# Moving one tile's attention under a different gather, and one tile's weighted sums onto one engine

## Chip, cores, metric

The kernel runs on one core of one Trainium2 chip. The metric is device time in microseconds (us) of one execution, the median over several runs. A core has five engines, each with a queue that it works through in order: TensorE (PE: matmuls; PEld is its weight loads), VectorE (DVE), ScalarE (ACT), GpSimd (POOL, which here only issues the gathers) and SyncE (SP, which issues all other transfers). Sixteen DMA engines move the data.

## The reference, cut to what matters

512 tokens of width 1024 go through two layers. The work is cut into four tiles of 128 tokens.

1. First layer, attention ("mix"): neighbourhood attention and grouped-query attention over all 512 tokens, two sigmoid gates (`ga`, `gb`), two projections, an output projection, added to the tokens.
2. First layer, PEER: each token picks 8 heads x 16 = 128 of 16,384 experts by two rounds of top-16, and adds the gated sum over them:

```python
uc = u[ic]                                            # 128 rows of 1024 for each token
act = einsum("cd,ced->ce", xc, uc)
hid = gelu(act) * gc
out = einsum("ce,ced->cd", hid, v[ic])                # 128 more rows of 1024
```

3. Second layer: a gated state-space block with short convolutions and dense projections (below: "block C"), over the tiles in order.

All inputs are fp32. The rows of `u` and `v` lie side by side, so one gather fetches, for each of 128 tokens, one row of 2048 floats: 128 x 8 KB = 1.049 MB. There are 4 x 128 = 512 such gathers, 537 MB in all.

## The kernel before, in words

**Stages.** `mix_first` does keys and values of all tokens and attention of tile 0. Then `queries` ranks tile 0's experts. `mix_rest([1, 2, 3])` does attention of the other three tiles together: each weight block is loaded once and multiplied with 384 columns (q, `ga`, `gb` and `pj` blocks), then `merge` projects. Then `queries` of tile 1, `queries` of tiles 2 and 3 together (256 columns), the ranking of tiles 2 and 3, and block C for tiles 0 and 1 (`block_c([0, 1])`). When that is through, `T.drain()` does what gathers are left, and `block_c([2, 3])` runs alone.

**The gathers** run beside all this. `peers` is a generator: one step issues two gathers (L269) and all that hangs on them. For each gather: VectorE multiplies the `u` half with the token and sums it up (L271), ScalarE takes Gelu (L276), VectorE makes a diagonal matrix `dg` of the weight (L280), and TensorE multiplies it with the `v` half into two banks of PSUM (L285). `acc` stands for these sums. Four matmuls of 64 x 64 by 512 columns stand for one gather of tiles 1 to 3; each fp32 matmul is two records in the trace, so a gather is eight records.

**Tile 0 is done another way.** A pair of gathers shares four matmuls, which take only the first 512 columns of both `v` rows. The other 512 columns are summed on VectorE into `own` (L295), with weights `hid` (L289):

```python
V.scalar_tensor_tensor(own, g[:, 1, HALVES[1]], hid[:, j:j + 1], own, op0=OP.mult, op1=OP.add)
```

**Pace.** `Paced` counts the columns that TensorE is given (four for one in fp32) and takes a step of `peers` each time `every` columns are full: `PACE_B` during `mix_rest` and tile 1's `queries`, `PACE_Q` during the queries of tiles 2 and 3, `PACE_C` in block C. In the ranking of tiles 2 and 3, `T.steps_now(3)` takes three steps after each head. Then `while 1 not in pre: T.steps_now(1)` takes steps until tile 1's sums have been added to the tokens (`folded`), which the first matmul of block C (`xbc`) needs. A gather needs a free buffer of six (`g`), and buffers come free when the last reader is through.

**Order.** The Tile scheduler reorders what is near; the order on each engine is then fixed. Constants of block C (`cw`, `cb`, `ssn` and others) are loaded when the ranking's memory comes free.

## Time and profile before

| | us |
|---|---|
| median of 3 runs | 2217.51 |
| lowest, highest | 2215.78, 2218.11 |
| the profiled execution, its own time | 2217.67 |
| its span in the trace | 2215.8 |

The page of the profile gives, over the span: PE busy 1851.5 us (84%), DVE 1628.1 (73%), ACT 735.1 (33%), POOL 598.8 (27%); 711.71 MB moved. A busy share is an average over stages with different limits, so the trace is best read in stretches cut where the kernel's stages change. In such a row, the POOL count after 204 us is the number of gathers issued there, since POOL issues nothing else.

### The profile page before, as it was taken

The numbers are of one execution on the slowest core, as the hardware profiler recorded it, in microseconds if no ns is written. First come the engines' busy times: TensorE is split into PE (matmuls) and PEld (weight loads), VectorE is DVE, ScalarE is ACT, GpSimd is POOL, SyncE is SP. The second block draws the span as 40 slices with busy tenths as digits, with TensorE's granted clock in tenths as the row PEclk, the third lists the DMA queues.
The fourth block names the chain that finished last, engine by engine and source line by source line (L and its number), as shares of the span: only waits on it lengthen the run. The fifth ranks groups of instructions, "written<-read, shape, count | busy, mean of one in ns | idle before, by whom it ended". The sixth has DMA issues, their size and how long they took to land.

```text
span 2215.8 us, 29509 instructions
## 1 busy us (share of the span) xinstructions
PE 1851.5 (84%) x10292; PEld 1032.5 (47%) x10292; DVE 1628.1 (73%) x4007; ACT 735.1 (33%) x1471; POOL 598.8 (27%) x520
## 2 busy tenths in 40 slices
PE   7998699899999898656648886896899866799998
PEld 5767445444444654001104552462453421298896
DVE  5376986788885966888868887886775766687865
ACT  4374265566501421111123342321220310154443
POOL 0000223333331233444433334433423333200000
PEclk9999789999999998656758997998999976699999
DMA  5366979889997899999989989899999999653363
GB/s 211 127 228 216 363 288 344 335 325 350 346 381 273 316 378 394 380 380 397 362 306 346 418 365 396 335 418 420 406 415 416 402 416 421 276 170 97 119 189 121
DMA packets 127316, 711.71 MB, mean 321 GB/s; under 512 B 15168, under 2 KB 18752, under 8 KB 61248
## 3 DMA queue, kind: packets, MB, share of 16 engines
q0 software_dynamic: 73728, 536.90, 60.6%
q1 hardware_dynamic: 53440, 172.92, 22.1%
q8 instruction: 83, 1.36, 0.2%
q14 instruction: 65, 0.53, 0.1%
HBM read 707.67 MB, written 2.10 MB: 320 GB/s over the span
## 4 chain that ended last, share of the span: by engine, by line
PE 36%; DMA 25%; DVE 24%; issue 7%; ACT 6%; POOL 1%; another core or an unknown queue 0%; DVEq 0%; POOLq 0%; ACTq 0%; SPq 0%
DMA g<-in_uv,idx 23%; DVE g L271 9%; PE sc L168 5%; PE acc L285 4%; PE mix L168 3%; PE pq L168 2%; PE ga L168 2%; PE z L168 2%; DVE dg L280 2%; PE pg L168 2%; PE ys L168 2%; DVE ww L354 2%; POOL g L269 1%; DVE own L295 1%; PE xbc L168 1%
## 5 line engine op out<-in xcount | busy, mean ns | idle before, releaser
L269 POOL DMA_INDIRECT g<-in_uv,idx x512 | 595.0, 1162 | 1297.7 <-PE acc L285 610.2
L285 PE MATMUL acc<-g,dg 64*64 64x512 f32 x3584 | 626.5, 755 | 249.9 <-DVE dg L280 229.8
L271 DVE SCALAR_TENSOR_TENSOR g<-g,xnp 128x1024 f32<-128x1024 f32 x512 | 624.7, 1221 | 188.2 <-DMA g<-in_uv,idx 181.9
L285 PEld LDWEIGHTS acc<-g,dg 64*64 64x64 f32 x3584 | 122.9, 154 | 621.0 <-DVE dg L280 492.8
L276 ACT ACTIVATE act<-act 128x1 f32<-128x1 f32 (+1 forms) x448 | 90.8, 203 | 945.7 <-DVE g L271 912.2
L354 DVE TENSOR_TENSOR ww<-w,ww 128x1024 fp32r<-128x1024 f32 x175 | 213.4, 1222 | 76.4 <-ACT ww L353 74.5
L280 DVE TENSOR_SCALAR dg<-two,act,gate 128x64 f32<-128x64 f32 x512 | 172.1, 351 | 132.6 <-ACT act L276 129.9
L353 ACT CAST ww<-w 128x1024 fp32r<-128x1024 f32 x175 | 182.2, 1044 | 172.8 <-PE sc L168 63.6
L168 PEld LDWEIGHTS sc<-hT,ww 128*128 128x128 f32 x1536 | 190.0, 193 | 54.0 <-issue 44.5
L168 PE MATMUL sc<-hT,ww 128*128 128x256 f32 x1536 | 206.1, 289 | 6.0 <-ACT fold L333 3.2
L168 PE MATMUL pq<-xT,w 128*128 128x128 f32 (+1 forms) x768 | 127.8, 323 | 0.6 <-DMA w<-in_wq 0.6
L168 PEld LDWEIGHTS pq<-xT,w 128*128 128x128 f32 x768 | 112.0, 200 | 19.8 <-issue 12.2
L295 DVE SCALAR_TENSOR_TENSOR own<-g,hid,own 128x512 f32<-128x512 f32 x127 | 95.1, 749 | 2.3
L168 PE MATMUL ga<-h,w 128*128 128x384 f32 x256 | 93.1, 513 | 2.8 <-DVE rot L411 2.8
L276 ACT ACT_TABLE_LOAD x61 | 78.3, 1283 | 18.1 <-DVE g L271 16.3
L168 PE MATMUL xbc<-hT,ww 128*128 128x256 f32 x480 | 64.2, 290 | 6.2 <-DVE ww L354 3.3
L168 PEld LDWEIGHTS xbc<-hT,ww 128*128 128x128 f32 x480 | 59.3, 192 | 20.4 <-issue 9.5
L168 PEld LDWEIGHTS ga<-h,w 128*128 128x128 f32 x256 | 48.7, 198 | 37.6 <-issue 8.3
L168 PE MATMUL q<-h,w 128*128 128x128 f32 (+1 forms) x256 | 61.1, 394 | 3.4 <-ACT rsq L407 3.4
L168 PE MATMUL mix<-w,ycat 128*128 128x512 f32 x128 | 61.5, 612 | 0.0
L168 PEld LDWEIGHTS z<-hT,ww 128*128 128x128 f32 x384 | 46.9, 190 | 12.3 <-issue 10.5
L168 PE MATMUL z<-hT,ww 128*128 128x256 f32 x384 | 50.5, 287 | 1.5 <-ACT raw L928 1.3
(338 smaller groups left out, 2269.8 us busy)
## 6 DMA issues: line engine op xcount, KB each, us to landing
w<-in_w SPq DMA_DIRECT2D x100, 512.0 KB
w<-in_wq SPq DMA_DIRECT2D x48, 512.0 KB
w<-in_wo SPq DMA_DIRECT2D x32, 512.0 KB
w<-in_wgm SPq DMA_DIRECT2D x16, 512.0 KB
w<-in_wout SPq DMA_DIRECT2D x16, 512.0 KB
g<-in_uv,idx POOLq DMA_INDIRECT x512
w<-in_wpg SPq DMA_DIRECT2D x16, 512.0 KB
w<-in_wqa SPq DMA_DIRECT2D x8, 512.0 KB
```

The source lines that it names most:

```text
L168: return self.count(max(n, 128) * (4 if rhs.dtype == F32 else 1), self.tensor.matmul(out, lhsT, rhs, **kw))
L269: G.indirect_dma_start(out=g.rearrange("p a d -> p (a d)"), out_offset=None, in_=a["uv"], in_offset=bass.IndirectOffsetOnAxis(ap=hk_idx[t] ...
L271: V.scalar_tensor_tensor(g[:, 0, :], g[:, 0, :], 1.0, xnp, op0=OP.mult, op1=OP.mult, accum_out=act[:, j % grp:j % grp + 1])
L276: A.activation(act[:, :grp], act[:, :grp], AF.Gelu)
L280: V.tensor_scalar(dg[:, m, :], two[:, 1, :], act[:, m:m + 1], gate[:, m:m + 1], op0=OP.mult, op1=OP.mult)
L285: T.tensor.matmul(acc[i][o, :], w, v, start=(e0 + j + 1 == grp), stop=(e0 + j + grp >= P), tile_position=(64 * i, 64 * m), skip_group_chec ...
L295: V.scalar_tensor_tensor(own, g[:, 1, HALVES[1]], hid[:, j:j + 1], own, op0=OP.mult, op1=OP.add)
L353: A.copy(ww[:, 0], w)
L354: V.tensor_tensor(ww[:, 1], w, ww[:, 0], op=OP.subtract)
```

## The change

- `mix_rest([1, 2])` (256 columns) stands where `mix_rest([1, 2, 3])` stood; `queries` of tile 1 follows at the same pace `PACE_B`; then `mix_rest([3])` (128 columns) at pace `PACE_Q`. Weights of the mix (`wqa`, `wqb`, `wga`, `wgb`, `wproj`, `wout`) are loaded a second time for tile 3.
- The paces are 10700, 8270 and 4950 instead of 13600, 10500 and 4600.
- Tile 0's sums are done as those of the others: four matmuls for each gather; `own` and `hid` are gone, and so is the form of `folded` for them.
- The ranking of tiles 2 and 3 takes 28 steps instead of 48, and its first two calls of `best` take two heads each.

```diff
-    first, rest = [0], [1, 2, 3]
+    first, late = [0], [2, 3]
-    PACE_B, PACE_Q, PACE_C = 13600, 10500, 4600
+    PACE_B, PACE_Q, PACE_C = 10700, 8270, 4950
...
-                        for m in range(grp):
-                            V.tensor_scalar(dg[:, m, :], two[:, 1, :], act[:, m:m + 1], gate[:, m:m + 1], op0=OP.mult, op1=OP.mult)
-                        for m in range(2):
-                            for i in range(2):
-                                r, o = slice(64 * i, 64 * i + 64), slice(64 * m, 64 * m + 64)
-                                w, v = (dg[r, m, :], gs[m][r, 1, HALVES[0]]) if grp == 2 else (dg[r, 0, :], g[r, 1, HALVES[m]])
...
-                    if t == 0:
-                        hid = sm.tile([P, 2], F32, tag="hid", name="hid", bufs=4)
-                        V.tensor_tensor(hid, act, gate, op=OP.mult)
-                        for j, g in enumerate(gs):
...
-                                V.scalar_tensor_tensor(own, g[:, 1, HALVES[1]], hid[:, j:j + 1], own, op0=OP.mult, op1=OP.add)
...
+                    V.scalar_tensor_tensor(g[:, 0, :], g[:, 0, :], 1.0, xnp, op0=OP.mult, op1=OP.mult, accum_out=act)
+                    A.activation(act, act, AF.Gelu)
+                    dg = dgs()
+                    V.tensor_scalar(dg[:, 0, :], two[:, 1, :], act, hk_gate[t][:, e:e + 1], op0=OP.mult, op1=OP.mult)
+                    for k in range(2):
+                        for i in range(2):
+                            r, o = slice(64 * i, 64 * i + 64), slice(64 * k, 64 * k + 64)
+                            T.tensor.matmul(acc[i][o, :], dg[r, 0, :], g[r, 1, HALVES[k]], start=(e == 0), stop=(e == P - 1),
+                                            tile_position=(64 * i, 64 * k), skip_group_check=True)
...
-                mix_rest(rest, h2)
-        late = rest[1:]
+                mix_rest([1, 2], h2[:, :, 0:2 * P])
+                with pool("pr") as pr, pool("p3") as pw:
+                    queries(pw, [1], [(h, 2, [1]) for h in (0, 2, 4, 6)], lambda *x: ranked(pr, *x))
+                T.every = PACE_Q
+                mix_rest([3], h2[:, :, 2 * P:])
         with pool("p4") as pw:
-            with pool("p5") as pq:
-                queries(pq, rest[:1], [(h, 2, rest[:1]) for h in (0, 2, 4, 6)], lambda *x: ranked(pw, *x))
-            T.every = PACE_Q
...
-            for t in late:
-                for h in range(8):
...
-                    T.steps_now(3)
+            for t, runs in zip(late, ((2, 2, 4), (4, 4))):
+                h = 0
+                for n in runs:
+                    f = firsts(pw, f"{h % 8}")
+                    for m in range(n):
...
+                        T.steps_now(2 - (t == late[0] and m % 2))
+                    best(pw, t, f, h, n)
+                    h += n
```

How the orders differ at three places. First VectorE, in the attention stage beside tile 0's gather; before:

```order
453 L271 SCALAR_TENSOR_TENSOR g,act<-g,xnp 128x1024
454 L624 ISA s,mx<-s,nab 128x512
455 L624 ISA mx 128x1
456 L271 SCALAR_TENSOR_TENSOR g,act<-g,xnp 128x1024
457 L627 RECIPROCAL nm<-nm 128x1
458 L280 TENSOR_SCALAR dg<-two,act,gate 128x64 x2
459 L289 TENSOR_TENSOR hid<-act,gate 128x2
460 L295 SCALAR_TENSOR_TENSOR own<-g,hid,own 128x512 x2
```

and after:

```order
461 L264 SCALAR_TENSOR_TENSOR g,act<-g,xnp 128x1024
462 L267 TENSOR_SCALAR dg<-two,act,gate 128x64
463 L264 SCALAR_TENSOR_TENSOR g,act<-g,xnp 128x1024
464 L267 TENSOR_SCALAR dg<-two,act,gate 128x64
465 L264 SCALAR_TENSOR_TENSOR g,act<-g,xnp 128x1024
466 L384 SCALAR_TENSOR_TENSOR raw<-raw,gqk,rope 128x256
```

`hid` and `own` are gone, and each `dg` (now L267) stands alone behind its own sum (now L264), before that of the next gather.

Second TensorE, at the end of the merge (`xo`) and the start of tile 1's query blocks (`pq`); before:

```order
364 L168 MATMUL xo<-w,mT 128x512 x12
365 L285 MATMUL acc<-g,dg 64x512 x4
366 L168 MATMUL xo<-w,mT 128x512 x8
367 L171 MATMUL tr<-idn,scr 128x128 x8
368 L168 MATMUL pq<-xT,w 128x128 x24
369 L168 MATMUL sc<-subk,q 128x128 x2
370 L168 MATMUL pq<-xT,w 128x128 x8
```

and after:

```order
332 L168 MATMUL xo<-w,mT 128x512 x3
333 L271 MATMUL acc<-g,dg 64x512 x11
334 L171 MATMUL tr<-idn,scr 128x128 x8
335 L271 MATMUL acc<-g,dg 64x512 x13
336 L168 MATMUL pq<-xT,w 128x128 x16
337 L271 MATMUL acc<-g,dg 64x512 x4
338 L168 MATMUL pq<-xT,w 128x128 x16
```

Before, tile 1's queries hold no gather work; after, tile 0's last gathers (`acc`, now L271) stand between them.

Third TensorE, from the last score block of tiles 2 and 3 (`sc`) to the first `xbc` of block C; before:

```order
440 L168 MATMUL sc<-subk,q 128x128 x8
441 L285 MATMUL acc<-g,dg 64x512 x400
442 L321 MATMUL fold<-parts,two 64x512 x4
443 L285 MATMUL acc<-g,dg 64x512 x14
444 L171 MATMUL tr<-idn,scr 128x128 x8
445 L285 MATMUL acc<-g,dg 64x512 x16
446 L171 MATMUL tr<-idn,scr 128x128 x8
447 L285 MATMUL acc<-g,dg 64x512 x12
448 L168 MATMUL xbc<-hT_7735,ww 128x256
```

and after:

```order
600 L168 MATMUL sc<-subk,q 128x128 x2
601 L271 MATMUL acc<-g,dg 64x512 x180
602 L298 MATMUL fold<-parts,two 64x512 x4
603 L271 MATMUL acc<-g,dg 64x512 x60
604 L171 MATMUL tr<-idn,scr 128x128 x8
605 L271 MATMUL acc<-g,dg 64x512 x12
606 L168 MATMUL dt<-wd,hT_8662 128x16 x2
607 L171 MATMUL tr<-idn,scr 128x128 x8
608 L271 MATMUL acc<-g,dg 64x512 x12
609 L168 MATMUL xbc<-hT_8662,ww 128x256 x48
```

Between the last scores and the first `xbc` stood 442 matmuls of gathers, and now stand 264; tile 1's `fold` has moved away from the `xbc`, back into the ranking.

## Rows read from the trace of the kernel before

**Rows 1.** The page: share of DMA and rate in 40 slices.

```profile
DMA  5366979889997899999989989899999999653363
GB/s 211 127 228 216 363 288 344 335 325 350 346 381 273 316 378 394 380 380 397 362 306 346 418 365 396 335 418 420 406 415 416 402 416 421 276 170 97 119 189 121
```

**Rows 2.** Stretches: each engine's busy us (instructions), granted PE clock, DMA share, rate.

```profile
204.00:285.00 81.00, 60.71 (x362) 44.60 (x360) 70.03 (x354) 25.78 (x52) 18.89 (x16) 0.80 0.88 328
285.00:707.00 422.00, 395.12 (x1742) 187.91 (x1740) 326.00 (x715) 196.74 (x348) 129.54 (x112) 0.97 0.87 333
707.00:791.00 84.00, 68.85 (x474) 53.74 (x476) 67.54 (x339) 39.32 (x76) 16.83 (x15) 0.94 0.89 335
791.00:865.00 74.00, 72.59 (x412) 47.54 (x408) 38.79 (x88) 10.67 (x42) 22.32 (x21) 0.98 0.95 371
865.00:1120.00 255.00, 154.45 (x744) 25.38 (x735) 214.66 (x730) 36.53 (x134) 113.28 (x92) 0.64 0.96 385
1120.00:1186.00 66.00, 34.58 (x172) 10.28 (x171) 46.00 (x97) 17.14 (x42) 23.36 (x18) 0.67 0.83 301
1186.00:1775.00 589.00, 509.31 (x3197) 269.03 (x3201) 446.11 (x918) 163.99 (x365) 217.31 (x186) 0.93 0.98 396
1775.00:1923.00 148.00, 99.92 (x492) 20.65 (x484) 92.06 (x173) 16.93 (x63) 53.49 (x52) 0.72 0.97 403
1923.00:2215.80 292.80, 278.83 (x1870) 242.80 (x1866) 208.16 (x406) 130.50 (x197) 0.00 (x0) 0.97 0.43 135
```

**Rows 3.** The page: DMA queues, packets, bytes, share of 16 engines' span.

```profile
q0 software_dynamic: 73728, 536.90, 60.6%
q1 hardware_dynamic: 53440, 172.92, 22.1%
```

**Rows 4.** Groups of instructions, whole execution: busy us, mean ns, idle before.

```profile
L271 DVE SCALAR_TENSOR_TENSOR g<-g,xnp 128x1024 f32<-128x1024 f32 x512 | 624.7, 1221 | 188.2 <-DMA g<-in_uv,idx 181.9 <-PE acc L285 4.0 <-PE pq L168 1.3
L280 DVE TENSOR_SCALAR dg<-two,act,gate 128x64 f32<-128x64 f32 x512 | 172.1, 351 | 132.6 <-ACT act L276 129.9 <-issue 2.4
L295 DVE SCALAR_TENSOR_TENSOR own<-g,hid,own 128x512 f32<-128x512 f32 x127 | 95.1, 749 | 2.3
```

**Rows 5.** TensorE groups by shape, 285 to 707 us.

```profile
L168 PE MATMUL ga<-h,w 128*128 128x384 f32 x256 | 93.1, 513 | 2.8 <-DVE rot L411 2.8
L285 PE MATMUL acc<-g,dg 64*64 64x512 f32 x472 | 76.4, 623 | 6.9 <-DVE dg L280 6.2 <-DVE hid L289 0.7
L168 PE MATMUL pj<-yT,w 128*128 128x384 f32 x128 | 44.0, 493 | 2.2 <-DVE gb L677 2.2
```

**Rows 6.** TensorE groups by shape, 707 to 865 us.

```profile
L168 PE MATMUL pq<-xT,w 128*128 128x256 f32 x256 | 63.3, 401 | 0.0
```

**Rows 7.** Timeline of TensorE: two groups of eight records, back to back.

```profile
680.90 1.95 PE L285 MATMUL acc<-g,dg 64*64 64x512 f32 x16
```

**Rows 8.** Timeline of POOL, issue of gathers: start, us, [idle before].

```profile
683.95 1.50 POOL L269 DMA_INDIRECT g<-in_uv,idx  x1 [0.30 <-issue]
739.19 0.94 POOL L269 DMA_INDIRECT g<-in_uv,idx  x1 [53.74 <-issue]
```

**Rows 9.** Waits, 285 to 592 us: total us, times, longest.

```profile
POOL g L269 <- PE acc L285: 111.7, 19, 13.3
POOL g L269 <- DVE own L295: 42.7, 8, 10.0
```

**Rows 10.** Timeline of VectorE before block C.

```profile
1140.66 0.18 DVE L863 TENSOR_SCALAR cw<-cw 128x40 f32<-128x40 f32 x1 [5.20 <-DMA cw<-in_cw]
...
1144.81 0.17 DVE L863 TENSOR_SCALAR ssn<-ssn 128x8 f32<-128x8 f32 x1 [3.81 <-DMA ssn<-in_ssn]
```

**Rows 11.** Timeline of TensorE: first matmul of block C.

```profile
1185.58 0.38 PE L168 MATMUL xbc<-hT,ww 128*128 128x256 f32 x1 [0.66 <-ACT hT L882]
```

**Rows 12.** DMA issues: times issued, KB each.

```profile
w<-in_wqa SPq DMA_DIRECT2D x8, 512.0 KB
...
nab<-in_nab SPq DMA_DIRECT2D x8, 384.0 KB
```

**Rows 13.** Timeline of TensorE: first q block of tile 0's attention.

```profile
86.45 3.73 PE L168 MATMUL q<-h,w 128*128 128x128 f32 x32
```

More of the change, by code (lines that the diff above doesn't have):

```diff
@@ L222, in program @@
         V.tensor_tensor(two[:, 1, :], idn[:, 0:64], idn[:, 64:128], op=OP.add)
-        folds = [two[:, 1:3, :], two[:, 0:2, :]]
         xres = keep.tile([P, NT, D], F32, tag="xres", name="xres")
@@ L256, in peers @@
                 V.scalar_tensor_tensor(xnp, xres[:, t, :], xn[t], row[0], op0=OP.mult, op1=OP.mult)
-                parts = done and evacuated(done[0])
+                parts = done and evacuated(done)
                 acc = [ps.tile([P, 512], F32, tag=f"a{i}", name="acc") for i in range(2)]
-                own = None
-                for e0 in range(0, P, 2):
-                    while len(hk_idx[t]) < e0 + 2:
+                for e in range(P):
+                    while len(hk_idx[t]) <= e:
@@ L296, in peers @@
-                    if parts is not None:
-                        folded(t - 1, parts, done[1])
-                        parts = None
-                    yield
-                done = acc, own
-            A.activation(col("rt"), act[:, 0:1], AF.Sqrt, bias=eps, scale=0.0)
-            folded(t, evacuated(acc), own)
+                    act = sm.tile([P, 1], F32, tag="act", name="act", bufs=4)
+                    g = gp.tile([P, 2, D], F32, tag="g", name="g")
+                    G.indirect_dma_start(out=g.rearrange("p a d -> p (a d)"), out_offset=None, in_=a["uv"],
+                                         in_offset=bass.IndirectOffsetOnAxis(ap=hk_idx[t][e], axis=0))
@@ L305, in dgs @@
+                    if e % 2:
+                        if parts is not None:
+                            folded(t - 1, parts)
+                            parts = None
+                        yield
+                done = acc
+            A.activation(col("rt"), act, AF.Sqrt, bias=eps, scale=0.0)
+            folded(t, evacuated(acc))
         def dgs():
@@ L312, in evacuated, with folded @@
             return parts
[L314 to L316 removed]
+        def folded(t, parts):
+            acc = [bank("fold", "sb") for _ in range(2)]
             for i in range(2):
[L318 to L324 removed]
+                for k in range(2):
+                    r, o = slice(64 * k, 64 * k + 64), slice(64 * i, 64 * i + 64)
+                    T.tensor.matmul(acc[k][o, :], two[r, 1, :], parts[r, i, :], start=True, stop=True,
+                                    tile_position=(64 * k, 64 * i), skip_group_check=True)
             xt = xres[:, t, :]
@@ L505, in spread @@
                         def spread(u):
-                            if u < 8:
-                                gate(u, a["wga"], mT)
-                            if 12 <= u < 20:
-                                if not gb:
-                                    gb.append(pa.tile([P, 8, n], F32, tag="kv", name="gb"))
-                                gate(u - 12, a["wgb"], gb[0])
+                            each = 2 if len(tiles) == 1 else 1
+                            kind, v = divmod(u, 4 * len(tiles))
+                            if kind and not gb:
+                                last = tiles[-1] == NT - 1
+                                gb.append((pa if last else py).tile([P, 8, n], F32, tag="kv" if last else "gb", name="gb"))
+                            for i in range(each * v, min(each * v + each, 8)):
+                                gate(i, a["wgb" if kind else "wga"], gb[0] if kind else mT)
                         def put(i, b):
```

43 lines of the change are left out of this document (4 added, 39 removed).

## The prediction

> **What bounds the kernel now.** I read the page's slices first. The DMA row [rows 1] shows 7 to 9 tenths in every slice from the fifth (222 us) to the thirty-fourth (1883 us), and mostly 3 to 6 before and behind. So the first question in each stage is whether DMA is full there, and the rate in GB/s is the measure. Next I cut the span at the kernel's stages [rows 2]. The reader is to see four things.
>
> - From 1186 to 1923 us (block C of tiles 0 and 1, then the drain) DMA stands at 0.98 and 0.97, 396 and 403 GB/s, with 186 + 52 gathers issued. TensorE is at 86% and VectorE at 76% in block C. This half of the kernel is bound by DMA, and the last part (293 us) starts when the last gather is through.
> - From 285 to 707 us (attention of three tiles) DMA gets 333 GB/s only: TensorE is busy 395 of 422 us. TensorE sets this stage.
> - From 707 to 791 us gathers pause: POOL issues none for 53.74 us [rows 8], and the rate is 335 GB/s.
> - From 865 to 1120 us (ranking) DMA has 0.96 and VectorE 215 of 255 us; from 1120 to 1186 us the rate drops to 301 GB/s, with VectorE held for 5.20 and 3.81 us by loads of constants [rows 10].
>
> So what lies ahead of the first `xbc` at 1186 us [rows 11] decides: the time of this matmul, and how many gathers are behind it by then. In TensorE's order 268 gathers stand ahead of it before, and 280 after.
>
> **The break-even.** Block C and the drain have 12 gathers fewer after the change. They are DMA-bound, so each is worth 1.049 MB at 396 GB/s = 2.65 us [rows 2]; 12 give back 32 us. The kernel is therefore faster if the first `xbc` comes before 1186 + 32 = 1218 us, and slower behind it.
>
> **What is removed and added.** VectorE loses 128 `own` instructions of 0.749 us, 95.1 us in all [rows 4], and `hid`. TensorE gets 64 more groups of eight records; two back to back take 1.95 us, so 0.97 us each [rows 7], 62 us in all. DMA gets 40 more weight blocks of 512 KB (4 + 4 of `wqa`, `wqb`, 8 each of the other four; one shown in [rows 12]) and 1.6 MB more of the bias table (eight pieces of 384 KB become eight of 320 and eight of 256): 22.5 MB. ScalarE gets 64 more Gelu instructions; it is busy 197 of 422 us [rows 2], which hides them. The order does what the change says: gathers now stand in tile 1's queries, and tile 1's `fold` is away from the `xbc`. I add up the stages to the first `xbc`, with gathers counted in TensorE's order.
>
> **Up to 285 us** nothing moves but some `own` instructions; 285.
>
> **Attention of tiles 1 and 2** (gathers 6 to 98: 93). TensorE sets it. Its 395 us hold 59 groups of gathers (472 records [rows 5]) at 0.97 us, 57 us; 338 us are attention. Of these 137 us are `ga` and `pj` at 384 columns, 364 ns a record for `ga`; at 256 columns a record is 247 ns [rows 6], so 137 becomes 93. The other 201 us go by tiles, to 134. Together 227, with 93 groups of gathers (each gather now has its own) 90 more: 317 us. TensorE was idle for 27 us of the old stage; two thirds are 18. Sum 335 us. The bytes, 93 gathers, 21.0 MB of weights and 2.6 MB of table, are 121 MB, 361 GB/s, below what block C gets, so DMA doesn't set it. Bounds: 317 with no idle time, and 374 if a group costs 76.4 / 59 = 1.29 us [rows 5] and all 27 us stay idle. I take the back-to-back price, since TensorE is nearly full. VectorE has 93 x (1.22 + 0.35) = 146 us of gather work here [rows 4] instead of 59 pairs with `own`: off the path, as it was at 326 of 422.
>
> **Tile 1's queries, attention of tile 3, queries of tiles 2 and 3** (gathers 99 to 214: 116). 116 gathers are 121.6 MB; two sets of query weights (16 blocks) and keys (1 MB) 18.9 MB; tile 3's weights and table 23.1 MB. 163.6 MB. TensorE has some 113 us for tile 3 (338 / 3), about 106 for queries (the 141 us from 707 to 865 less the 36 gathers issued there at 0.97) and 113 for gathers: 333 us. DMA is the longer one. Rates that I have: 371 GB/s beside queries, 396 in block C, 403 in the drain [rows 2]. I take 391, near block C, since most of these bytes are of the same mix of gathers and weights: 418 us. Bounds 406 (at 403) and 441 (at 371). The weights that are read again cost 21 MB, 54 us of this.
>
> The Trainium skill, "DMA: Bandwidth & Descriptors", Specifications, states a limit of about 358 GB/s from HBM for a core. The trace differs: 396 GB/s over 589 us and 403 over 148 [rows 2]. By the page's figure this stage would be 457 us and the whole 2277; I go by the measured rates.
>
> **Ranking of tiles 2 and 3** (gathers 215 to 275: 61). VectorE: in 865 to 1120 us, 92 gathers at 1.57 us are 144 of 215 us, so 70 us are ranking [rows 2, 4]; with 61 gathers, 96 + 70 and tile 1's addition to the tokens, some 6 us: 172. DMA: 64 MB at that stretch's 385 GB/s, 166. Two engines nearly equal, each waiting on the other; I take 178. Bounds 166, and 205 if VectorE stays at 84%, its share there now.
>
> **To the first `xbc`** (5 gathers). The loads of constants stand at the same place in VectorE's order: 5.20 + 3.81 us again [rows 10], and 5 x 2.65. 22 us; bounds 13 and 27 (at 66 / 18 = 3.7 us a gather, as from 1120 to 1186, and the wait). Tile 1's sums, which stood ahead of the `xbc` before, are done by then.
>
> **Sum.** 285 + 335 + 418 + 178 + 22 = 1238 us, 52 later than 1186; less 32 for the 12 gathers: 20 us slower. Behind that nothing changes: the last 293 us stay. The profiled execution took 2217.67 us (span 2215.8), 0.16 above the median. 2238 us.
>
> **Why the gain isn't larger.** The 95 us of `own` lay on an engine that had 96 us to spare in its stage; the DMA idle time that can be filled, from 204 to 1186 us, is about 99 us by the shares [rows 2], and 55 of these lie in the attention stage (0.87), which stays TensorE's.
>
> **Rivals.**
> - *The buffers come free sooner* (ends faster). POOL waited 42.7 us for `own` to release buffers, but 111.7 us for TensorE [rows 9]. If this release is what starves DMA, the attention stage runs at its 317, the next ones at the drain's rate, 406, and ranking at 166: 285 + 317 + 406 + 166 + 22 = 1196, 22 us faster, 2196 us. It decides below 1218. Against it: TensorE's 93% in the stage, and the larger wait. Chance 0.21.
> - *The weights ride free* on SP's queue: 22.5 MB at 396 GB/s are 57 us less, 2181 us. Against it: gathers and weights together take 60.6 + 22.1% of the span of all engines [rows 3], and DMA is at 0.98 where both run. The Trainium skill, same page, "Issuing engines are not separate DMA queues", says that transfers from SP and GpSimd run on the same 16 engines and interleave; by that the reread costs its bytes, and the 0.98 agrees. Chance 0.05.
> - *Attention of one tile waits on itself.* Tile 0's attention alone took from 86 [rows 13] to 204 us, 118 us with no gather. If tile 3's 61 gathers come on top of such a chain at 2.65 us, 118 + 162 = 280 us instead of about 220 (87 MB at 396): 60 more, 2298 us. Against it: gates and gathers stand between its steps. Chance 0.10.
> - *Even:* the pause of 53.74 us and the hole from 1120 to 1186, both filled, pay for the weights: 2217 us. Chance 0.12.
>
> **Numbers.** The forecast has 0.52 and its own range is 2223 to 2275. About 0.2%, 4.4 us, is what a measurement of this kernel can tell from no change. Faster: 0.21 + 0.05 = 0.26; same 0.12; slower 0.52 + 0.10 = 0.62. The bounds of the terms reach 18, 12, 12 and 9 us below (attention, queries, ranking, start of block C) and 39, 23, 27 and 5 above; all at one end is unlikely. I take 2195 to 2280: it leaves out the free weights, the one-tile chain and the ends.
>
> **What would show it.** `own` gone from VectorE; no pause in POOL before 1186 us. TensorE over 93% and about 360 GB/s in the first attention stage, ending near 620 us; near 390 GB/s from there to about 1040; first `xbc` near 1238 us with 280 gathers ahead of it; block C at 0.98 and shorter by some 27 us. The prediction is wrong if the first `xbc` comes before 1218 us, if attention of tiles 1 and 2 takes under 317 us, or if tile 3's stage shows DMA under 0.9 with TensorE waiting on VectorE or ScalarE.

## The result and the profile after

The change takes 2307.44 us (median of 4 runs, 2305.99 to 2312.62) against 2217.81 us beside it: a ratio of 1.0402, 95% interval 1.0374 to 1.0431. It is 4.0% slower, some 90 us; forecast were 2238 us, 20 us more than before. The profiled execution took 2307.45 us, its span is 2305.7 us.

The page's slices and queues, as in [rows 1, 3]:

```profile
DMA  5466978888998989999869899879999999833353
GB/s 203 131 225 228 372 294 326 328 330 337 353 412 323 350 311 418 418 415 411 321 241 355 343 417 373 330 282 418 416 416 416 398 376 416 373 124 120 119 183 119
q0 software_dynamic: 73728, 536.90, 58.2%
q1 hardware_dynamic: 60352, 195.47, 23.5%
```

q1 has grown by 22.5 MB, the weights and bias tables that are read again. Stretches of the changed kernel, cut at its stages (columns as in [rows 2]; the POOL count is gathers issued):

```profile
285.00:620.00 335.00, 312.29 (x1664) 166.71 (x1663) 181.32 (x391) 142.18 (x292) 96.36 (x85) 0.96 0.86 330
620.00:714.00 94.00, 79.09 (x503) 47.37 (x501) 66.04 (x278) 21.61 (x54) 24.87 (x25) 0.87 0.91 361
714.00:952.00 238.00, 202.36 (x1298) 109.85 (x1298) 148.00 (x383) 94.97 (x205) 71.16 (x61) 0.93 0.93 366
952.00:1055.00 103.00, 102.38 (x582) 61.51 (x583) 52.48 (x101) 22.49 (x64) 38.51 (x32) 1.00 1.01 416
1055.00:1250.00 195.00, 105.12 (x476) 18.94 (x475) 173.16 (x694) 39.86 (x121) 66.08 (x59) 0.59 0.84 328
1250.00:1281.00 31.00, 17.61 (x83) 5.06 (x83) 22.62 (x47) 8.43 (x19) 11.04 (x8) 0.59 0.89 319
1281.00:1858.00 577.00, 502.24 (x3089) 266.59 (x3090) 426.30 (x881) 158.60 (x350) 207.73 (x175) 0.91 0.94 381
1858.00:2014.00 156.00, 102.58 (x505) 23.37 (x503) 96.99 (x180) 16.52 (x62) 57.92 (x53) 0.73 0.97 398
2014.00:2305.70 291.70, 275.36 (x1870) 239.44 (x1866) 205.65 (x405) 132.15 (x200) 0.00 (x0) 0.97 0.40 131
```

In order: attention of tiles 1 and 2, queries of tile 1, attention of tile 3, queries of tiles 2 and 3, ranking, constants, block C, drain, last block. The first `xbc`, which stood at 1185.58 us [rows 11]:

```profile
1280.85 0.38 PE L168 MATMUL xbc<-hT,ww 128*128 128x256 f32 x1 [0.65 <-ACT act L265]
```

Set against the working of the prediction, three lines make up the 69 us that it lacked:

| | forecast | measured |
|---|---|---|
| up to the end of attention of tiles 1 and 2 | 620 | 620 |
| from there to the end of the late queries | 418 | 435 |
| ranking and start of block C | 200 | 226 |
| first `xbc` to the end of the span | 998 | 1025 |

The last line is 1030 us before (2215.8 - 1185.6); the 12 gathers fewer were to give back 32 us and gave back 5.

To see where a kernel loses, the best measure is the gathers themselves. This table shows when VectorE starts the k-th sum of a gather (rows of L264 in the timeline, L271 before, in order, counted from 0): first the time in us before, then how much later (+) or earlier (-) the others are. The names are those of the experiments below.

| k | before | change | sums alone | old sums | move alone | ranking alone | ranking, old pace |
|---|---|---|---|---|---|---|---|
| 98 | 596.4 | +15.6 | +53.5 | +10.3 | +9.7 | -3.1 | +0.7 |
| 128 | 749.7 | -7.4 | +74.9 | -18.8 | -17.7 | -6.5 | +0.2 |
| 214 | 1012.4 | +41.8 | +76.9 | +4.7 | +6.2 | +17.3 | +24.7 |
| 258 | 1149.9 | +47.1 | +76.0 | +12.5 | -11.5 | +1.5 | +9.1 |
| 300 | 1288.4 | +61.5 | +74.7 | +25.7 | -23.1 | +6.4 | +14.4 |
| 380 | 1534.3 | +82.1 | +77.2 | +52.0 | -22.0 | +32.7 | +15.7 |
| 459 | 1787.2 | +82.4 | +76.8 | +52.5 | -11.9 | +38.0 | +14.7 |
| 511 | 1919.2 | +93.6 | +76.3 | +64.1 | +7.6 | +34.5 | +16.4 |

Block C is where the change should have won and did not: from k = 300 to 380 it loses 21 us more. A stretch of it shows how. Of the changed kernel, three windows of block C's state-space part for tiles 0 and 1:

```profile
1421.00:1450.00 29.00, 19.69 (x102) 3.35 (x99) 19.90 (x38) 3.49 (x13) 16.12 (x13) 0.71 1.01 415
1461.00:1500.00 39.00, 25.42 (x137) 10.84 (x129) 28.42 (x76) 14.55 (x28) 12.75 (x12) 0.78 0.76 286
1500.00:1525.00 25.00, 22.93 (x83) 10.43 (x87) 11.25 (x25) 5.77 (x9) 2.06 (x2) 0.52 0.43 181
```

In the first, twelve gathers stand in TensorE's order between the matmul of the state (`st`) and that of the norm (`sn`) of tile 0, and nothing else does: TensorE takes them as they land, DMA is full, and block C stands still. In the third, tile 1's state-space matmuls (`ys`, below "the strip") run, with two gathers issued: DMA is at 0.43. The granted clock is 0.52 there, close to the lower level, 1.2 GHz; ahead of it TensorE was idle a third of the time. The strip alone, in the change and in the kernel before:

```profile
1503.00:1523.00 20.00, 19.29 (x66) 8.88 (x62) 7.51 (x16) 2.94 (x5) 1.78 (x1) 0.50 0.39 163
```

```profile
1405.00:1418.00 13.00, 12.17 (x78) 6.15 (x78) 8.31 (x18) 3.02 (x6) 3.75 (x3) 1.00 0.70 268
```

The clock is 0.50 in one and 1.00 in the other. Two `ys` rows of the change, and two of the kernel before:

```profile
1505.28 0.69 PE L168 MATMUL ys<-m,xd 128*64 128x128 f32 x2
1505.90 0.69 PE L168 MATMUL ys<-cs,st 64*64 64x128 f32 x2
```

```profile
1406.60 0.43 PE L168 MATMUL ys<-m,xd 128*64 128x128 f32 x2
1406.96 0.43 PE L168 MATMUL ys<-cs,st 64*64 64x128 f32 x2
```

The strip therefore runs from 1503 to 1523 us, where it took from 1405 to 1418 us. DMA loses 39 x 0.24 + 25 x 0.57 = 24 us in the second and third window.

Two smaller holes. At tile 1's last gather, in the ranking, POOL waits 16.42 us, since tile 2's first sums need the banks that hold tile 1's, and the copies that empty them stand behind ranking work on VectorE, or wait for it. Of TensorE and POOL there:

```profile
1201.06 6.76 PE L271 MATMUL acc<-g,dg 64*64 64x512 f32 x24 [10.89 <-ACT parts L289]
```

```profile
1208.11 0.94 POOL L262 DMA_INDIRECT g<-in_uv,idx  x1 [16.42 <-PE acc L271]
```

At the start of the drain, VectorE waits for a weight block of the last part (`ww`), which stands ahead of a gather's sum in its order, and POOL waits with it. VectorE, then POOL:

```profile
1889.88 1.23 DVE L329 TENSOR_TENSOR ww<-w,ww 128x1024 fp32r<-128x1024 f32 x1 [9.85 <-ACT ww L328]
1891.02 1.22 DVE L264 SCALAR_TENSOR_TENSOR g<-g,xnp 128x1024 f32<-128x1024 f32 x1
```

```profile
1895.23 1.38 POOL L262 DMA_INDIRECT g<-in_uv,idx  x1 [11.92 <-PE acc L271]
```

In the table the 11 us from k = 459 to 511 go with it, nearly all of them by k = 467 (+93.0).

### The profile page after: what moved, and what is told of

Same layout as the page of the kernel before. It is cut to its first block, busy times and chain, and to the rows that moved or that the text cites. A ratio compares the mean times of both kernels' runs of the same rounds, so it can differ in the third digit from the quotient of the medians.

```text
span 2305.7 us, 31763 instructions
## 1 busy us (share of the span) xinstructions
PE 1939.2 (84%) x11336; PEld 1114.1 (48%) x11336; DVE 1558.1 (68%) x3900; ACT 759.2 (33%) x1575; POOL 594.8 (26%) x520
## 4 chain that ended last, share of the span: by engine, by line
PE 32%; DMA 25%; DVE 22%; issue 11%; ACT 6%; POOL 3%; SPq 0%; POOLq 0%; DVEq 0%; ACTq 0%
DMA g<-in_uv,idx 23%; DVE g L264 9%; PE sc L168 5%; PE acc L271 3%; PE mix L168 3%; POOL g L262 3%; PE z L168 2%; PE ys L168 2%; PE pg L168 2%; PE ga L168 2%; DVE ww L329 2%; PE s L168 1%; DVE dg L267 1%; PE mf L168 1%; PE xbc L168 1%
## 5 line engine op out<-in xcount | busy, mean ns | idle before, releaser
L271 PE MATMUL acc<-g,dg 64*64 64x512 f32 x4096 | 687.1, 724 | 250.2 <-DVE dg L267 227.5
L264 DVE SCALAR_TENSOR_TENSOR g<-g,xnp 128x1024 f32<-128x1024 f32 x512 | 624.9, 1221 | 275.4 <-DMA g<-in_uv,idx 250.3
L265 ACT ACTIVATE act<-act 128x1 f32<-128x1 f32 x512 | 103.8, 203 | 1007.9 <-DVE g L264 990.2
L271 PEld LDWEIGHTS acc<-g,dg 64*64 64x64 f32 x4096 | 137.0, 148 | 605.0 <-DVE dg L267 449.4
L267 DVE TENSOR_SCALAR dg<-two,act,gate 128x64 f32<-128x64 f32 x512 | 179.3, 350 | 166.8 <-ACT act L265 160.7
L168 PE MATMUL ga<-h,w 128*128 128x256 f32 (+1 forms) x512 | 100.6, 346 | 0.0
L168 PEld LDWEIGHTS ga<-h,w 128*128 128x128 f32 x512 | 80.0, 198 | 20.9 <-issue 14.9
L168 PE MATMUL q<-h,w 128*128 128x128 f32 (+1 forms) x384 | 69.0, 336 | 4.0 <-ACT rsq L382 4.0
L168 PEld LDWEIGHTS q<-h,w 128*128 128x128 f32 x384 | 59.1, 209 | 21.6 <-issue 12.4
L168 PE MATMUL mix<-w,ycat 128*128 128x512 f32 x128 | 61.5, 612 | 0.0
L168 PE MATMUL pj<-yT,w 128*128 128x256 f32 (+1 forms) x256 | 51.1, 352 | 4.2 <-DVE mT L654 3.3
L171 PE MATMUL pT<-idn,s 128*128 128x128 f32 x256 | 42.4, 292 | 12.3 <-DVE rot L386 10.8
```

Source lines behind the costliest of these rows:

```text
L168: return self.count(max(n, 128) * (4 if rhs.dtype == F32 else 1), self.tensor.matmul(out, lhsT, rhs, **kw))
L171: return self.count(4 * 128, self.tensor.transpose(out, src, identity))
L264: V.scalar_tensor_tensor(g[:, 0, :], g[:, 0, :], 1.0, xnp, op0=OP.mult, op1=OP.mult, accum_out=act)
L265: A.activation(act, act, AF.Gelu)
L267: V.tensor_scalar(dg[:, 0, :], two[:, 1, :], act, hk_gate[t][:, e:e + 1], op0=OP.mult, op1=OP.mult)
L271: T.tensor.matmul(acc[i][o, :], dg[r, 0, :], g[r, 1, HALVES[k]], start=(e == 0), stop=(e == P - 1), tile_position=(64 * i, 64 * k), skip_g ...
```

## The experiments

All medians, with the ratio to the kernel before:

| kernel | us | ratio, 95% interval |
|---|---|---|
| the change | 2307.44 | 1.0402 (1.0374 to 1.0431) |
| sums alone | 2294.54 | 1.0348 (1.0312 to 1.0384) |
| move alone | 2229.37 | 1.0049 (1.0032 to 1.0065) |
| move, no rereading | 2226.60 | 1.0046 (1.0022 to 1.0070) |
| ranking alone | 2256.12 | 1.0182 (1.0154 to 1.0210) |
| ranking, old pace | 2234.34 | 1.0082 (1.0049 to 1.0115) |
| change, old sums | 2275.04 | 1.0267 (1.0221 to 1.0314) |
| change, no rereading | 2293.40 | 1.0350 (1.0319 to 1.0382) |
| change, other banks | 2276.53 | 1.0265 (1.0238 to 1.0292) |
| change, old ranking | 2279.05 | 1.0273 (1.0246 to 1.0300) |
| change, old pace | 2298.77 | 1.0367 (1.0326 to 1.0408) |
| change, old sums, other banks | 2258.91 | 1.0179 (1.0150 to 1.0207) |
| change, old sums, no rereading | 2254.65 | 1.0163 (1.0137 to 1.0189) |
| before, other banks | 2218.73 | 1.0002 (0.9986 to 1.0018) |
| before, constants early | 2213.58 | 0.9978 (0.9963 to 0.9994) |
| move, constants early | 2226.06 | 1.0040 (1.0022 to 1.0058) |

### Tile 0's sums: alone, and taken back

Sums alone:

```diff
--- before
-                    grp = 2 if t == 0 else 1
+                    grp = 1
...
-                    if t == 0:
-                        hid = sm.tile([P, 2], F32, tag="hid", name="hid", bufs=4)
...
```

> The kernel before with one part of the change alone: tile 0's sums wholly on TensorE, nothing else. Theory of bytes: the pause of 54 us in POOL takes up most of the longer attention stage, 2218 to 2235 us. Theory of sums: attention of three tiles is TensorE's, so 62 us more there and nothing given back, 2260 to 2280 us.

The theory of sums has the right sign, and 77 us is more than it allowed; the theory of bytes falls. Of that kernel, the attention of three tiles (now 498 us long), and TensorE's group of gathers in it:

```profile
285.00:783.00 498.00, 459.86 (x2189) 206.10 (x2189) 243.35 (x517) 211.54 (x404) 116.67 (x111) 0.96 0.74 277
```

```profile
L285 PE MATMUL acc<-g,dg 64*64 64x512 f32 x924 | 142.8, 624 | 12.7 <-DVE dg L280 12.7
```

142.8 us for 924 records are 1.24 us a group of eight, not the 0.97 that I took from two groups back to back [rows 7]. 64 groups at that price are 79 us, and the table shows 75 us at k = 128 and the same from there to the end: nothing is made up. VectorE, freed of `own`, went from 326 of 422 us to 243 of 498; that bought nothing.

The price comes from the order, which cuts groups in two. Rows of the same stage of that kernel:

```profile
302.47 1.94 PE L285 MATMUL acc<-g,dg 64*64 64x512 f32 x14
304.34 0.66 PE L171 MATMUL pT<-idn,s 128*128 128x128 f32 x4
304.93 1.08 PE L285 MATMUL acc<-g,dg 64*64 64x512 f32 x6
```

```profile
360.44 1.07 PE L285 MATMUL acc<-g,dg 64*64 64x512 f32 x2
```

Two records on their own take 1.07 us, six take 1.08, and a whole group of eight 1.09. In this stage's timeline 47 of 69 runs of gather records are not a whole number of groups. Each part counted as a whole group, 115.5 groups become 141, and 142.8 us are 1.01 us for each of these.

A whole group that stands alone among other matmuls costs a little more than one behind another, 1.09 us in this row of the changed kernel:

```profile
1421.55 1.09 PE L271 MATMUL acc<-g,dg 64*64 64x512 f32 x8
```

The Trainium skill, "TensorEngine Tiling (Array Packing)", Key Properties, says that a change of the tiling mode drains TensorE; the row agrees in its sign, 1.09 against 0.97 us, and no run here separates that from other causes.

The other way round, the change with tile 0's `peers` and `folded` of before:

```diff
--- after
+                    grp = 2 if t == 0 else 1
...
+                                V.scalar_tensor_tensor(own, g[:, 1, HALVES[1]], hid[:, j:j + 1], own, op0=OP.mult, op1=OP.add)
```

> The changed kernel with tile 0's sums done as before: pairs of gathers on TensorE for 512 columns, own on VectorE for the others; attention, paces and ranking stay as changed. Theory of bytes (the weights read again cost their bytes, and little else counts): TensorE's saving of 62 us in the first two stages is hidden, 2295 to 2315 us. Theory of sums (64 more groups on a full TensorE are on the path): 30 to 60 us of the 90 come back, 2247 to 2277 us. If VectorE then holds the buffers, 2320 or more.

32 us come back, within the theory of sums. In the table this kernel is nearly level with before at k = 214 (+4.7), where the change is at +41.8. So up to the ranking the change loses by its sums; what this kernel still loses, 59 us, lies behind.

### The weights that are read again

Three kernels leave out 39 of the 40 weight blocks of tile 3: the change, the change with old sums, and the move alone (below).

```diff
+        once = {}
         def wtile(src, n):
+            if once:
+                return once["w"] if n == P else ...
...
+                once["w"] = ph.tile([P, 8, P], F32, tag="once", name="once")
+                SP.dma_start(once["w"], a["wga"][0])
                 mix_rest([3], h2[:, :, 2 * P:])
+                once.clear()
```

> The changed kernel, but the attention of tile 3 multiplies one weight block, loaded once, instead of reading its 40 blocks again (so the output for tile 3 is another one): 39 blocks of 512 KB, 20.4 MB, fewer. Theory of bytes: 20.4 MB at 0.39 MB/us, 52 us less, 2255 us, the stage of tile 3 shorter by 40 to 50 us. Theory of the chain (tile 3's attention waits on itself and would take as long without the loads): 2295 to 2310 us, the stage still 225 us or more.

> The changed kernel with tile 0's sums as before, and the attention of tile 3 with one weight block loaded once instead of its 40 read again (output of tile 3 another one); its order is free of the clump, too. Theory of the hidden bytes (with TensorE relieved, DMA is full in tile 3's stage, and 20.4 MB cost what they take): 35 to 52 us less than the kernel with the old sums and the other banks, 2200 to 2215 us. Theory of TensorE (the stage is set by its own chain): within 10 us of that kernel, 2240 to 2260 us.

> The kernel of the move alone, but the attention of tile 3 multiplies one weight block, loaded once, instead of reading 40 again (output of tile 3 another one). Theory of bytes: 35 to 52 us less than with the blocks. Theory of TensorE: within 12 us of it.

The theory of bytes, on which my sum rested, falls three times: 14, 4 and 3 us instead of 35 to 52. (The second is told by 2258.91 us, old sums with other banks, whose order in block C is nearly the same; against old sums, 2275.04 us, it is 20 us.) Even the 14 aren't the bytes': that kernel is only 2 us ahead of the change at k = 280 (+54.2 against +56.5), and its order in block C has no run of twelve gathers. In the other two pairs the bytes do show ahead of block C: at k = 280 old sums without the bytes is 12 us ahead of old sums (+10.2 against +22.3), and the move without them 11 us ahead of the move (-26.4 against -15.3). That is a fifth of the 54 us that I had put on them. The edit also changes the order, so none of the three takes away bytes alone. Tile 3's attention in the change and in the kernel without the 20.4 MB, from tile 1's last query block to the first late one:

```profile
711.00:954.00 243.00, 205.16 (x1320) 112.01 (x1319) 152.69 (x398) 97.33 (x209) 72.24 (x62) 0.93 0.93 367
```

```profile
717.00:961.00 244.00, 214.40 (x1366) 114.73 (x1366) 159.89 (x410) 103.39 (x219) 75.31 (x69) 0.93 0.81 310
```

The stage is as long, 243 and 244 us, with 69 gathers issued in it instead of 62; the DMA share falls from 0.93 to 0.81. I had read shares above 0.9 as "bound by DMA". Here they mostly weren't: what issues gathers is POOL, and POOL waits for TensorE to release buffers. Waits of the changed kernel from 285 to 1055 us:

```profile
POOL g L262 <- PE acc L271: 377.6, 115, 13.9
```

377.6 of 770 us, in 115 waits. The Trainium skill, "Perfetto Trace Analysis", Identifying the Most-Contended Engine, calls the occupancy of 16 DMA engines misleading and asks for HBM utilization, the rate against a peak, instead. The rows agree that the share misleads: 0.93 goes with 367 GB/s here, where the next stage (952 to 1055 us) shows 416.

### Buffers

If POOL waits for buffers, and TensorE for the weights (`dg`) of gathers that are late, the number of buffers could be the limit. I took the stretch from tile 1's queries to the late queries and changed the six buffers of the move alone (next section).

```diff
-                gp = gathering.enter_context(pool("gp", 6, side="right"))
+                gp = gathering.enter_context(pool("gp", 5, side="right"))
--- 7 buffers: 7 in place of 5, and
-                wws = [(pc, 2), (pc, 2)] + ([(px, 1)] if px else [])
+                wws = [(pc, 1), (pc, 1)] + ([(px, 1)] if px else [])
```

> The move alone with five buffers for gathers instead of six. Theory of the buffers (each gather of the stretch waits for the round of six, 3.6 us a gather): the stretch from tile 1's queries to the late queries gets 60 us or more longer, 500 us or more instead of 438, and the kernel takes over 2290 us. Theory of TensorE's order (waits are for work in order, not for buffers): the stretch stays within 15 us, and the kernel under 2260 us.

> The move alone with seven buffers for gathers; for the memory, block C splits its weights in one buffer instead of two, so that only what lies ahead of the first xbc is compared. Theory of the buffers: the stretch gets 25 us or more shorter for each gather's worth, 3.2 us or less a gather instead of 3.5. Theory of TensorE's order: as many us a gather as before, within 0.1.

The whole kernels took 2293.77 us and 2353.81 us (one execution each; the second has a slower block C by its own edit). The stretch in the change, and in the move alone with six, five and seven buffers:

```profile
620.00:1055.00 435.00, 383.83 (x2383) 218.72 (x2382) 266.52 (x760) 139.07 (x321) 134.54 (x118) 0.93 0.95 377
```

```profile
553.00:991.00 438.00, 358.49 (x2180) 211.69 (x2180) 296.73 (x831) 135.66 (x302) 137.92 (x119) 0.91 0.95 377
```

```profile
553.00:1028.00 475.00, 374.99 (x2197) 212.99 (x2194) 312.69 (x863) 129.33 (x297) 152.47 (x128) 0.86 0.93 364
```

```profile
567.00:1029.00 462.00, 378.43 (x2264) 224.80 (x2267) 302.20 (x863) 138.90 (x317) 140.79 (x126) 0.90 0.95 376
```

438 us for 119 gathers, 475 for 128, 462 for 126: 3.68, 3.71 and 3.67 us a gather (the change: 435 / 118 = 3.69). With five buffers the stretch is longer than the theory of the order allowed, and shorter than that of the buffers said, with nine gathers more issued in it; the price of a gather hardly moves either way. Its whole time, 2293.77 us, is one that the theory of buffers gave. But for this stretch that theory falls; five buffers cost their time in the attention of tiles 1 and 2 (k = 40 to 110: +9.3 to +56.5, where the move alone goes from +5.3 to +24.8) and in block C (k = 300 to 459: +15.2 to +43.7, against -23.1 to -11.9). With old sums TensorE is busy 358 us there and with new ones 384, and the stretch is the same. Without the weights' bytes it is a little less, 3.61 (change, 437 us for 121) and 3.53 (move, 466 for 132). What remains is the order on TensorE, in which each gather waits for its place and each matmul behind a gather for its `dg`; that is argued, not shown.

### The move alone

The kernel before with the two `mix_rest` and the paces 10700 and 8270; sums, ranking and pace 4600 as before.

```diff
--- before
-    PACE_B, PACE_Q, PACE_C = 13600, 10500, 4600
+    PACE_B, PACE_Q, PACE_C = 10700, 8270, 4600
...
-                mix_rest(rest, h2)
+                mix_rest([1, 2], h2[:, :, 0:2 * P])
+                with pool("pr") as pr, pool("p3") as pw:
+                    queries(pw, [1], [(h, 2, [1]) for h in (0, 2, 4, 6)], lambda *x: ranked(pr, *x))
+                T.every = PACE_Q
+                mix_rest([3], h2[:, :, 2 * P:])
```

> The move of attention alone, with the weights read again and the paces of the first two stages that go with it; tile 0's sums, the ranking of tiles 2 and 3 and the pace of block C are as in the kernel before. Theory of bytes: 22.5 MB more at 0.39 MB/us are paid in full, 2255 to 2275 us. Theory of TensorE (bytes hide where TensorE sets the pace; what costs is the sums, the ranking and the order in block C): 2218 to 2240 us.

11 us, in the range of the second theory, though not for its reason, as the buffers' section shows. The move does what it says: its gathers are 23 us ahead of the kernel before at k = 300, bytes and all. Block C and the drain take it back.

### Banks, and the run of gathers in block C

```diff
-                acc = [ps.tile([P, 512], F32, tag=f"a{i}", name="acc") for i in range(2)]
+                acc = [ps.tile([P, 512], F32, tag=f"{'a' if t < 2 else 'p'}{i}", name="acc") for i in range(2)]
...
-                tags = ["p1", "a0", "a1"] if last else ["sb", "p1"]
-                turns["mm"] = ["mm", "mm", "p0"]
+                tags = ["p1", "a0", "a1"] if last else ["sb", "a1"]
+                turns["mm"] = ["mm", "mm", "p0" if last else "a0"]
```

> The changed kernel with the sums of tiles 2 and 3 in two other banks of PSUM, so that tile 2's first sums need not wait until tile 1's have been copied out in the ranking. Theory of the seam (the hole of some 16 us at gather 256 delays all that follows): 2290 to 2297 us. Theory of bytes: DMA fills again behind the hole, 2302 to 2308 us.

> The changed kernel with tile 0's sums done as before and the sums of tiles 2 and 3 in two other banks. Its order has no run of twelve gathers between the state matmul and the norm of the state-space part of tile 0 any more. Theory of the clump (twelve gathers in a row there cost some 18 us, whatever the banks): gains add up, 2275 - 25 = 2245 to 2255 us. If the banks' gain of 31 us hung on tile 0's sums: 2270 to 2280 us.

> The kernel before with the sums of tiles 2 and 3 in two other banks, nothing else. Its order gets a run of thirteen gathers between dt and the cumulative sum of tile 1. Theory of the seam (a wait at gather 256 is removed): 2205 to 2212 us. Theory of the clump (a run of gathers inside the state-space part leaves the rest short): 2225 to 2240 us.

In the change, 31 us come back, more than either theory allowed. The trace says where: at k = 258 this kernel is 2.7 us ahead of the change (+44.4 against +47.1), at k = 268 it is 6.8 us ahead (+44.2 against +51.0), so the seam between tile 1's sums and tile 2's is worth some 4 us. From k = 300 to 380 it loses 4 us (+52.1 to +56.2) where the change loses 21. Its order has one gather between `st` and `sn` of tile 0, not twelve: other banks made the scheduler put them elsewhere, eleven in a row some 50 us ahead of tile 1's strip. With old sums the same sign: the two kernels differ by 16 us (2275.04 and 2258.91, the second between the ranges of its theories), and from k = 300 to 380 one loses 26 us and the other 12. On the kernel before the banks gain 4 us up to k = 280, and a new run of thirteen gathers in the state-space part of tile 1 takes 13 back from k = 320 to 360: no change at all. Both of its theories were half right.

The run of gathers has a rival as the cause: the clock in tile 1's strip. In seven kernels the strip, from the first `ys` to the last, takes 20 to 21 us at a granted clock of 0.50 to 0.65: the change; with old sums; with old sums and other banks; with old sums and no rereading; with the old pace; the ranking alone; and the kernel before with other banks. From k = 300 to 380, where the strip stands, these lose 10 to 26 us. In the kernel before and five others it takes about 13 us at 1.00 (sums alone; ranking, old pace; constants early; change, no rereading; change, other banks), and none of the five loses more than 4 us. (The kernels with the move and the old ranking have their strips near k = 380 or behind it and can't be compared.) The change with other banks has its run of eleven and a fast strip; old sums with other banks has no run longer than five there and a slow strip, and loses 12. So the loss goes with the strip's clock more closely than with a run of gathers. Whether a run lowers the clock, no experiment here separates.

### The ranking and its pace

The kernel before with the ranking of the change, once with its pace and once without; and the change with the ranking, or the pace, of before.

```diff
--- before (ranking alone)
-            for t in late:
-                for h in range(8):
...
-                    T.steps_now(3)
+            for t, runs in zip(late, ((2, 2, 4), (4, 4))):
...
+                        T.steps_now(2 - (t == late[0] and m % 2))
-    PACE_B, PACE_Q, PACE_C = 13600, 10500, 4600
+    PACE_B, PACE_Q, PACE_C = 13600, 10500, 4950
--- ranking, old pace: without the last pair of lines
```

> The kernel before with the ranking of the change alone (28 steps instead of 48, two calls of best with two heads) and its pace of block C, 4950. Theory of the ranking (it holds fewer gathers, so that VectorE sets it and DMA goes idle): 12 to 30 us slower than before, 2230 to 2248 us. Theory of TensorE and sums alone: 2215 to 2225 us, since the loop behind the ranking takes the steps that it lacks.

> The kernel before with the ranking of the change alone, the pace of block C left at 4600; TensorE's order from the first xbc on is that of before, gather by gather. Theory of the order in block C: the 38 us belong to pace 4950, which bunches ten gathers ahead of the state-space part of tile 1; 2217 to 2228 us. Theory of the ranking: 2245 us or more.

> The changed kernel with the ranking of tiles 2 and 3 as before: three steps after each head, two calls of best with four heads for each tile; 318 gathers instead of 280 then stand ahead of the first xbc. Theory of the ranking (VectorE sets it, and shorter runs of best cost more): 8 to 15 us faster than the change, 2292 to 2299 us. Theory of the block (gathers moved out of block C leave it short of them, so that DMA goes idle there): 2310 to 2330 us.

> The changed kernel with the pace of block C at 4600 as before. Its order then has eighteen gathers in a row between the norm of tile 0 and dt of tile 1, instead of twelve between state and norm. Theory of the order in block C: a bunch again, of another place, so 2290 to 2310 us. Theory of the pace itself (4950 gives block C too few gathers): 2270 to 2285 us.

The ranking alone costs 40 us, more than its theory allowed. At the old pace, where the order from the first `xbc` on is that of before, 18 of them stay: between the ranges of the two theories, so both have a part. 22 us go with the pace of 4950 and the order that it gives to block C. Of the ranking alone, two windows of tile 1's state-space part:

```profile
1380.00:1390.00 10.00, 6.65 (x25) 2.48 (x22) 7.98 (x28) 2.65 (x6) 1.51 (x1) 0.52 0.12 50
1412.00:1434.00 22.00, 20.35 (x76) 9.49 (x72) 10.38 (x21) 4.11 (x8) 2.08 (x2) 0.53 0.51 207
```

DMA is at 0.12 in the first and 0.51 in the second, where `ys` runs near the low clock again (0.53). The ranking's own 18 us: from 865 to 1120 us 84 gathers are issued instead of 92 [rows 2]:

```profile
865.00:1120.00 255.00, 145.45 (x673) 23.92 (x672) 209.41 (x748) 42.61 (x135) 99.09 (x84) 0.61 0.92 347
```

Taking the old ranking into the change gives 28 us back, both theories being off: it is ahead of the change by 48 us at k = 300 (+14.0) and by 33 at the end (+61.0); why block C and the drain take 15 us of it back is open. The old pace alone gives 9 us back; its order has eighteen gathers in a row, behind the norm instead of ahead of it, and the gathers from k = 340 to 360 still lose 20 us. A bunch elsewhere, as that theory had it.

### Constants loaded early

The kernel before, with eight small constants of block C loaded ahead of `mix_rest` instead of behind the ranking ([rows 10] shows the waits), and the move alone with the same.

```diff
--- before
+                tri = const("tri", [P, P], a["tri"])
...
+                ssn = const("ssn", [P, 8], a["ssn"])
+                A.activation(hd[:, 1, :], hd[:, 1, :], AF.Exp)
+                for half in (cw, cbias, ssn):
+                    V.tensor_scalar(half, half, 0.5, None, op0=OP.mult)
                 turns["y"] = ["p0", "p1"]
```

> The kernel before with eight small constants of block C (tri, seg, cw, cb, scw, hd, dsk, ssn) loaded ahead of the attention of the other tiles instead of behind the ranking; all else the same. If the waits of 5.20 and 3.81 us for these loads hold up the gathers, and what DMA loses there is not made up later: 5 to 10 us faster, 2207 to 2213 us. If DMA makes it up: 2216 to 2220 us.

> The move of attention alone, with the eight constants of block C loaded ahead of it. If what the early constants gain adds to the move: 5 to 10 us less than the move alone, 2219 to 2224 us. If DMA is full there now and the wait is covered: 2226 to 2232 us. To beat the kernel before and that with early constants it would have to come below 2208 us.

2213.58 us, 0.2% less than before, with an interval below 1: the lowest time here by a small margin, between the ranges of the two theories and at the edge of what can be told from no change. In its trace the gain is at the place itself: k = 255 is at +4.0 against before and k = 258 at -5.4; at k = 511 it is -2.3. On the move the same load gives 3 us, within the intervals of both, so it doesn't beat the kernel before.

## Why the prediction was wrong in size

- **The direction and its place were right.** TensorE set attention of tiles 1 and 2 (312 of 335 us), which ended at 620 us as forecast; `own` no longer stands on VectorE; the pause in POOL is gone, and from 285 us to the ranking no two issues start more than 16 us apart; the first `xbc` comes behind 1218 us, and by the break-even that decides. The 620 us are luck, two errors that cancel: 85 groups took 105.8 us (1.24 each), not 93 groups 90, and attention itself 206 us, not 227. Both come from one wrong price: at their own 76.4 us instead of 57 the 59 old groups leave 319 us of attention, which scale to 214. The rate there was 330 GB/s, not about 360.
- **The price of the sums was mis-sized.** 0.97 us a group from [rows 7]; 1.24 in the stage, where the order cuts groups and each part costs as much as a whole. I had the dearer price (1.29, [rows 5]) as the upper bound and chose the wrong end: 64 x 0.27 = 17 us. "TensorE is nearly full" spoke for the price of the same crowded stage, not for that of two groups standing together.
- **"DMA is the longer one", with 54 us for the bytes, was the wrong cause with a near result.** The stretch took 435 us (forecast 418, bounds 406 to 441), and without the bytes 437. Nor is it TensorE's (88% busy), nor the buffers': 3.67 to 3.71 us a gather with five, six and seven of them, and 3.53 to 3.61 without the bytes. Of the 54 us for the bytes 2 to 12 showed by k = 280; the rest filled DMA time that would be idle. *The weights ride free* was nearly right in its mechanism and wrong in its 2181 us: the time that the bytes don't cost is not time that the gathers gain.
- **Ranking: 226 us, not 200.** The upper bound of my two terms was 232. VectorE is busy 173 of 195 us there and DMA at 0.84: nearer to the case "VectorE stays at 84%" than to the 178 that I took. Its work was forecast well (172 us); that the stage would take little more than that was not. The seam of tile 1 to tile 2, moved into the ranking, is some 4 us of it; that the order showed `fold` there I noted, but not what waits behind it.
- **"Less 32 for the 12 gathers", and "behind that nothing changes", failed.** The rest took 1025 us, not 998, and block C ran at a DMA share of 0.94 (forecast 0.98). From k = 300 to 380 the change loses 21 us, with tile 1's strip at a clock of 0.50 and DMA idle for 24 us around it; that the run of twelve gathers is the cause is argued, not shown. The hole at the drain goes with another 11. I had costed the new pace at nothing, without looking at where it puts gathers between `st`, `sn` and `ys`: on the ranking alone it costs 22 us, in the change 9.
- **The rivals.** *Buffers free sooner* fell: POOL waits for TensorE, and taking `own` off VectorE alone, with its sums on TensorE, made the kernel 77 us slower. *One-tile attention waits on itself* gave 2298 us, near the result, by the wrong cause: tile 3's attention took 243 us with 62 gathers, not 280. *Even* holds for the move alone, nearly (11 us).

The kernels form a chain in which each differs from the one ahead of it by one part of the change: the move takes 11 us (2229.37, "move alone"), the ranking with its pace 46 us more (2275.04, "change, old sums", is the move with these two), the sums 32 us more (2307.44). So half of the loss is the ranking and the pace, of which the prediction had the ranking too short and the pace at nothing. Alone, the parts cost 11 us (move), 40 us (ranking with its pace) and 77 us (sums), 128 together. The difference is in the sums: beside attention of three tiles TensorE's 64 groups cost all of their 77 us, in the change 32, where part of them stand in a stretch that is as long without them. Not tried: gathers spread evenly in the state-space part by hand, and the drain's hole taken away alone. Open: what sets the 3.7 us a gather of that stretch, and what sets the clock of tile 1's strip.

## What to carry to other kernels

A DMA share of 0.93 beside a TensorE share of 0.85 (attention of tile 3) says that two limits are close, and not which one binds: ask who releases the buffers, look at the rate against the best rate of the same trace (416 GB/s here), and take bytes away once to see whether the stage gets shorter, counting the gathers in it. Price an instruction by its mean in the stage in which it will stand, not by two that stand together, and look for groups that the order cuts. A pace that is changed by 8% is a change of its own: compare the order of paced work in every place where its host has a serial stretch, and the granted clock and the DMA share of that stretch. To share out a loss among parts that meet, add them one by one, and not each alone: here 11, 46 and 32 us, where each alone costs 11, 40 and 77.

## What the runs showed of the hardware

- DMA moved 416 GB/s over 103 us (952 to 1055 us), with weights from SP's queue and gathers side by side.
- A part of a group of gather records costs as much as a whole one: two records 1.07 us, eight 1.09, in the attention of the kernel with sums alone.
- The granted clock was 0.59 in the ranking, where TensorE mostly follows gathers, busy 105 of 195 us. It was 0.50 in the change's strip, where TensorE was busy 19 of 20 us, behind 39 us in which it was idle a third. A pair of `ys` records takes 0.69 us at 0.50 against 0.43 at 1.00, and a group of eight gather records 1.99 us, as in this row of the changed kernel (clock 0.50 from 1186 to 1192 us), against 1.09:

```profile
1188.19 1.99 PE L271 MATMUL acc<-g,dg 64*64 64x512 f32 x8 [3.23 <-DVE dg L267]
```

The Trainium skill, "TensorE: Matmul & The Clock Gate", What's actually happening, gives 1.2 and 2.4 GHz as the two levels; the ratio of the second pair, 1.83, is near their ratio, that of `ys`, 1.6, is less.
